# A diff-attention and convolution block on one core: seven-product pairs in the first gate/up block too, a fifth pair in the ten others, pair sums split between VectorE and GpSimd

## The chip, the cores and the metric

One core of one Trainium2 chip runs the whole block. The metric is the device time of one execution in microseconds, median of three runs. In the profile, PE is TensorE, DVE is VectorE, ACT is ScalarE, POOL is GpSimd, SP is SyncE (it issues the weight loads).

## The reference

One layer of 256 rows and 2048 columns, all in fp32. What matters for the change is the second half, the feed-forward part.

```python
h = h + jnp.einsum('bsm,md->bsd', mixed, w_out[l])        # output projection, 2048 x 2048
hn = rms_norm(h, norm2_g[l])                              # h * rstd2(row) * g2(column)
a = jnp.einsum('bsd,df->bsf', hn, w_gate[l])              # 2048 x 5632
bu = jnp.einsum('bsd,df->bsf', hn, w_up[l])               # 2048 x 5632
h = h + jnp.einsum('bsf,fd->bsd', jax.nn.silu(a) * bu, w_down[l])   # 5632 x 2048
```

Ahead of it stand a norm, an input projection to 5120 columns, differential attention with four heads, and a gated causal convolution of 31 taps over 1024 channels; `mixed` is the two side by side.

## The kernel before

**Three products for one.** TensorE multiplies in a reduced format, so each fp32 operand is split in two: `hi`, the operand cast (ScalarE, for weights), and `lo`, the rest that the cast leaves (VectorE: raw minus hi). A product is hi·hi + hi·lo + lo·hi, three matmuls. Weights therefore come in as `raw` (SP's queue), become `whi` (line 326) and `wlo` (line 335), and are multiplied. For some units the rest is made by DMA instead: ScalarE writes the negated cast's operand and GpSimd's queue adds the raw tile to it (lines 329 and 330, "by DMA" below). A load of two k-tiles (256 rows) by 512 columns is one chunk; tiles of the activations (`xhi`, `hhi`, `chi`, `ahi`) are the stationary side, weights the moving side with 512 columns.

**Gate and up in blocks of 512 columns.** The feed-forward part goes through eleven blocks j of 512 hidden columns, in groups of four, four and three; behind each group stand passes over W_down for that group (`down_pass`). A block multiplies the 256 rows by 512 columns of W_gate and the same 512 of W_up over 16 k-tiles. Except in block 0 it saves products in the manner of Strassen: two k-tiles of both weights, which are 2x2 blocks (two k-tiles by gate and up; two halves of the rows by two k-tiles), are multiplied with seven products in place of eight. Such a unit is a pair, kind "s": 21 matmuls where two plain two-k-tile units, kinds "g" and "u", have 12 each. The seven products land in eight banks of PSUM (`PRODUCTS`, `sum_bank`), into which the plain units of the block add as well; behind the last pair the banks are combined (`bank_sums`: a copy by ScalarE, line 1186, and six sums by VectorE, lines 1188 to 1193); then silu, two more sums behind the last unit (line 1209), two products (line 1214), and transposes of the result (line 898). The sevenfold operands of the activations (`fhi`, `flo`) are made once by `make_forms`.

**What a pair needs.** Its four raw tiles `wb` (two loads of 512 KB); four sums or differences of them, `wt` (lines 1049 to 1051, the third reads the second's result); two casts on ScalarE, of the three tiles used as they are (line 1052, 1536 columns) and of the four summed ones (line 1055, 2048 columns); two rests on VectorE, `wlb` (line 1058) and `wlt` (line 1059). `wb`, `wh`, `wlb` and `wlt` have two buffers each, `wt` has one.

**Block 0** is plain, because the norm's row scale `rstd2` isn't known when it starts: its 16 chunks (192 matmuls) multiply `h` times the column gains, and `rstd2` scales the sums (lines 876 and 883). Meanwhile `make_forms` spreads `rstd2` over the partitions (two transposes), scales the transposed `hn` with it, and makes the seven forms of the scaled rows.

**Order.** All units stand in one list, and `run_chunks` goes through it: ahead of unit t's matmuls it writes the casts of units up to `hi_lead` further and the rests up to `lo_lead` further (3 and 2 in the feed-forward part), loads whatever has a free buffer, and advances the side work (generators such as `bank_sums`) one step at each `resume()` that the multiplications contain. So each engine's order is the order of writing. Within a block the order of units is a string:

```python
ORDER = "sggsggsuusuu"
FIRST_ORDER = "gsggsgsuusuu"
BY_DMA = dict(g=TWOS[:2], u=TWOS[1::2])
```

Four pairs, four "g" and four "u", 180 matmuls; of the eight plain units four have their rests made by DMA, in the first block of a group only the two "u" ones.

Of the kernel before, what the change touches and what calls it, by code (L numbers as in the profile page):

```python
# [12 lines left out]
F32 = mybir.dt.float32  # L13
# [20 lines left out]
LINE = 128  # L34
EPS = 1e-6
# [29 lines left out]
RAW_BUFS = 5  # L65
# [27 lines left out]
DORDERS = {4: (ORDER, ORDER), 3: ("gguusggsuu", "gsgsgsuuu")}  # L93
# [10 lines left out]
PAIR_BUFS = 2  # L104

# [24 lines left out]
def tile_block(  # L130
# [13 lines left out]
    prestack = ExitStack()  # L144
    pre = prestack.enter_context(tc.tile_pool(name="pre", bufs=2))
    small = prestack.enter_context(tc.tile_pool(name="small", bufs=4))
# [4 lines left out]
    h = [pre.tile([P, D], F32, tag=f"h{m}", name=f"h{m}", bufs=1) for m in range(NM)]  # L151
# [255 lines left out]
    def run_chunks():  # L407
# [4 lines left out]
        loaded, split = set(), set()  # L412
# [8 lines left out]
        def split_next():  # L421
            chunks[j]["split"](chunks[j])
            split.add(j)

# [3 lines left out]
        def freed(side, t):  # L428

            which, bufs = ((raws, RAW_BUFS), (pairs, PAIR_BUFS))[side]  # L430
            if not ahead[side] or pairs[2] - 1 not in loaded:
                return None
            k = which[place[side][ahead[side][0]] - bufs]
            return k if k in split and (t >= k or not chunks[k]["by_dma"]) else None

# [7 lines left out]
        for t in range(n):  # L443
# [33 lines left out]
    def square_sum(src, accum, **kw):  # L477
        junk = pre.tile([P, N], F32, tag="junk", name="junk", bufs=1)
# [107 lines left out]
    def conv_back(b):  # L586
# [37 lines left out]
        for b in range(2):  # L624
            for t in range(NB // 2):
# [6 lines left out]
                for j in range(2):  # L632
# [3 lines left out]
                    hi = pre.tile([P, S], F32R, tag="mchi", name=f"mchi{ct}", bufs=NCT)  # L636
                    lo = pre.tile([P, S], F32R, tag="mclo", name=f"mclo{ct}", bufs=NCT)
# [135 lines left out]
    def attend_values(hd):  # L773
# [39 lines left out]
    hT = {}  # L813

    hn = []
# [9 lines left out]
    def out_done(n, ps):  # L825
        cs = slice(n * N, (n + 1) * N)
# [13 lines left out]
        for t in range(0, N // P, 2):  # L840
# [6 lines left out]
            if k % HK == 0:  # L847
                hn.append(early.tile([P, HK, S], F32, tag="wb", name="hn"))
            rows = hn[k // HK][:, k % HK : k % HK + 2, :]
            for i in range(2):  # L850
                act.activation(rows[:, i, :], pt[:, i, :], AF.Copy, scale=col("g2", k + i))
            hi, lo = lhs_two("h", k)
            act.copy(hi, rows)
            dve.tensor_tensor(lo, rows, hi.bitcast(F32), ALU.subtract)
            for i in range(2):
                hT[k + i] = (hi[:, i, :], lo[:, i, :])
# [3 lines left out]
        else:  # L860
            yield
            yield
            prestack.close()
            ffn["pool"] = ctx.enter_context(tc.tile_pool(name="ffn", bufs=1))
            start(make_forms())


    ffn = {}
    actT = {}
    sil = {}  # L870

    def silu_done(ps):
        yield
        for m in range(NM):
            sil[m] = ffn["pool"].tile([P, N], F32, tag=f"sum{m}", name="sil")
            act.activation(sil[m], ps[m], AF.Silu, scale=rstd2[m])

    def up_done(j, ps):
        fp = ffn["pool"]
        aa = []  # L880
        for m in range(NM):
            a = fp.tile([P, N], F32, tag=f"sum{2 + m}", name="a")
            dve.scalar_tensor_tensor(a, ps[m], rstd2[m], sil[m], ALU.mult, ALU.mult)
            aa.append(a)
        yield from lag(4)
        yield from transposed(j, aa)

    def transposed(j, aa):
        last = j + 1 in FIRSTS and NDS[group_of(j)[0]] < HD
        b = j - group_of(j)[1]  # L890
        for t in range(N // P // 2):
# [9 lines left out]
            if b < 2 and 2 * t < nd:  # L901
                if not b and not t:
                    raw_act[g] = ffn["pool"].tile([P, 2, nd, S], F32, tag="draw", name="raw_act")
# [30 lines left out]
    def make_down_forms(g):  # L934
# [20 lines left out]
        hs = ffn["pool"].tile([P, 2, nd, P], F32R, tag="dhs", name="dhs")  # L955
# [12 lines left out]
        ls = ffn["pool"].tile([P, 4, nd, P], F32R, tag="draw", name="dls")  # L968
# [11 lines left out]
    def make_forms():  # L980
        fp = ffn["pool"]
        rep = fp.tile([P, S], F32, tag="sum1", name="rep")
        for m in range(NM):
            act.activation(rep[:, m * P : (m + 1) * P], ident, AF.Identity, bias=rstd2[m], scale=0.0)
        yield
        ps = aux_ps.tile([P, N], F32, tag="aux", name="ps_r")
        for m in range(NM):
            pe.transpose(ps[:, m * P : (m + 1) * P], rep[:, m * P : (m + 1) * P], ident)
        yield
        rb = fp.tile([P, S], F32, tag="sum2", name="rb")  # L990
        act.copy(rb, ps[:, :S])
        yield
        for i in range(2):
            for k in range(0, HK, 4):
                t = hn[i][:, k : k + 4, :]
                dve.tensor_tensor(t, t, rb.unsqueeze(1).to_broadcast([P, 4, S]), ALU.mult)
                yield

        nr = HK - NS
        chi = fp.tile([P, 2 * nr, S], F32R, tag="chi", name="chi")  # L1000
        clo = fp.tile([P, 2 * nr, S], F32R, tag="clo", name="clo")
# [374 lines left out]
```

## Time and profile before

| What | Value |
|---|---|
| median of three runs | 1032.45 us (1032.17, 1032.45, 1032.88) |
| the profiled execution, first to last instruction | 1030.8 us (the page gives no other time for it) |
| TensorE busy | 1025.7 us, 100% |
| VectorE busy | 929.2 us, 90% |
| ScalarE busy | 643.4 us, 62% |
| GpSimd busy | 102.7 us, 10% |
| TensorE's granted clock | 1.000 over the span |
| gate/up begins, first bank copies (line 1186) | 338.3 us; 419.8 us |

The span counts from the first to the last instruction; the runs' times are longer by what lies around it, here 1.65 us for the median. The page's busy time counts an instruction from start to end, and ends of pipelined matmuls are modelled, so 100% says that TensorE always has a matmul in flight. In a view of groups or times a row reads: line, engine, operation, out<-in, shape, and in brackets the idle time ahead of it with what ended it. In the view of windows each engine has a busy time and in brackets its number of instructions, in the order PE, PEld, DVE, ACT, POOL, then the granted clock, the DMA engines' share and GB/s.

### The profile page before, as it was taken

How to read it: one execution, taken by the hardware profiler on the slowest of the kernel's cores; microseconds unless marked ns; L12 is line 12 of the kernel's file. 1: busy time of each engine (PE TensorE's matmuls, PEld its weight loads, DVE VectorE, ACT ScalarE, POOL GpSimd, SP SyncE). 2: the span in 40 equal slices, each digit the busy share in tenths (PEclk: the TensorE clock that was granted, in tenths of full speed). 3: DMA queues.
4: the chain of work that ended last, by engine and by line, in shares of the span. 5: the costliest groups of instructions: out<-in, count | busy, mean ns of one | idle time of the engine just before them, and what ended most of it. 6: DMA issues, size and time to landing. Idle time of an engine off the chain costs nothing.

```text
span 1030.8 us, 13034 instructions
## 1 busy us (share of the span) xinstructions
PE 1025.7 (100%) x4642; PEld 849.4 (82%) x4642; DVE 929.2 (90%) x1128; ACT 643.4 (62%) x786; POOL 102.7 (10%) x146
## 2 busy tenths in 40 slices
PE   9999999999999999999999999999999999999998
PEld 8888888888888888888888888888888888888887
DVE  6899999999765699999999898989999989889998
ACT  7644656665756675676666556667757556657562
POOL 0300112111000000100102101101001111010020
PEclk9999999999999999999999999999999999999999
DMA  9757555544466677997989799889798979897776
GB/s 338 254 194 258 190 184 164 158 169 166 141 215 214 197 262 222 282 265 210 254 259 272 251 257 270 258 234 262 228 269 255 285 207 283 247 267 218 226 200 174
DMA packets 116448, 238.64 MB, mean 232 GB/s; under 512 B 7840, under 2 KB 9120, under 8 KB 116384
## 3 DMA queue, kind: packets, MB, share of 16 engines
q1 hardware_dynamic: 105216, 203.58, 59.3%
q0 software_dynamic: 10880, 34.08, 17.0%
q8 instruction: 36, 0.59, 0.2%
q14 instruction: 28, 0.23, 0.1%
q10 hardware_dynamic: 288, 0.16, 0.1%
HBM read 204.24 MB, written 9.44 MB: 207 GB/s over the span
## 4 chain that ended last, share of the span: by engine, by line
PE 100%; POOL 0%; DVE 0%; issue 0%; POOLq 0%
PE acc L365 11%; PE acc L366 11%; PE acc L371 11%; PE q L1097 11%; PE q L1103 11%; PE q L1098 11%; PE q L1078 9%; PE q L1077 9%; PE q L1076 9%; PE ps_a L898 1%; PE ps_s L712 1%; PE ps_o L782 1%; PE ps_warm L164 0%; PE ps_h L846 0%; PE ps_qk L693 0%; PE ps_at L802 0%
## 5 line engine op out<-in xcount | busy, mean ns | idle before, releaser
L326 ACT CAST whi<-raw 128x1024 fp32r<-128x1024 f32 (+1 forms) x256 | 264.2, 1043 | 143.8 <-PE acc L366 86.6
L335 DVE TENSOR_TENSOR wlo<-raw,whi 128x1024 fp32r<-128x1024 f32 (+1 forms) x208 | 250.4, 1214 | 38.2 <-ACT whi L326 38.0
L1055 ACT CAST wh<-wt 128x2048 fp32r<-128x2048 f32 x61 | 116.8, 1915 | 109.9 <-DVE wt L1051 109.7
L1059 DVE TENSOR_TENSOR wlt<-wt,wh 128x2048 fp32r<-128x2048 f32 x61 | 139.8, 2291 | 19.8 <-ACT wh L1055 19.7
L1097 PE MATMUL q<-whi,chi 128*128 128x512 f32 x320 | 125.2, 391 | 0.0
L1098 PE MATMUL q<-whi,clo 128*128 128x512 f32 x320 | 124.6, 389 | 0.0
L365 PE MATMUL acc<-whi,xhi 128*128 128x512 f32 x312 | 124.1, 398 | 0.0
L366 PE MATMUL acc<-whi,xlo 128*128 128x512 f32 x312 | 122.2, 392 | 0.0
L1076 PE MATMUL q<-wh,fhi 128*128 128x512 f32 x280 | 109.8, 392 | 0.0
L1077 PE MATMUL q<-wh,flo 128*128 128x512 f32 x280 | 109.0, 389 | 0.0
L1058 DVE TENSOR_TENSOR wlb<-wb,wh 128x1536 fp32r<-128x1536 f32 x61 | 106.8, 1751 | 1.0 <-ACT wh L1052 1.0
L572 DVE SCALAR_TENSOR_TENSOR y<-upad,cw,y 128x256 f32<-128x256 f32 x240 | 101.6, 490 | 0.0
L330 POOL DMA_DIRECT2D wlo<-raw x48 | 41.5, 865 | 555.7 <-ACT wlo L329 286.3
L1052 ACT CAST wh<-wb 128x1536 fp32r<-128x1536 f32 x61 | 89.8, 1472 | 1.0 <-DMA wb<-in_w_down_dram 1.0
L1103 PE MATMUL q<-wlo,chi 128*128 128x512 f32 x320 | 85.7, 390 | 0.0
L371 PE MATMUL acc<-wlo,xhi 128*128 128x512 f32 x312 | 85.2, 394 | 0.0
L1049 DVE TENSOR_TENSOR wt<-wb 128x1024 f32<-128x1024 f32 x61 | 74.4, 1220 | 0.0
L1097 PE MATMUL q<-whi,ahi 128*128 128x512 f32 x182 | 71.0, 390 | 0.0
L1098 PE MATMUL q<-whi,alo 128*128 128x512 f32 x182 | 70.9, 389 | 0.0
L1103 PEld LDWEIGHTS q<-wlo,chi 128*128 128x128 f32 x320 | 60.0, 188 | 12.7 <-DMA wlo<-raw 0.3
L1097 PEld LDWEIGHTS q<-whi,chi 128*128 128x128 f32 x320 | 60.1, 188 | 12.3
L1098 PEld LDWEIGHTS q<-whi,clo 128*128 128x128 f32 x320 | 60.1, 188 | 12.2
(260 smaller groups left out, 1850.5 us busy)
## 6 DMA issues: line engine op xcount, KB each, us to landing
raw<-in_w_in_dram SPq DMA_DIRECT2D x78, 512.0 KB, 4.6
raw<-in_w_gate_dram SPq DMA_DIRECT2D x48, 512.0 KB, 5.0
raw<-in_w_up_dram SPq DMA_DIRECT2D x48, 512.0 KB, 5.3
wlo<-raw POOLq DMA_DIRECT2D x48, 512.0 KB, 7.1
raw<-in_w_down_dram SPq DMA_DIRECT2D x46, 512.0 KB, 6.2
wb<-in_w_down_dram SPq DMA_DIRECT2D x42, 512.0 KB, 5.9
wb<-in_w_up_dram SPq DMA_DIRECT2D x40, 512.0 KB, 4.4
wb<-in_w_gate_dram SPq DMA_DIRECT2D x40, 512.0 KB, 5.5
```

Source lines behind the costliest of these rows:

```text
L326: act.copy(c["hi"], c["raw"])
L335: dve.tensor_tensor(c["lo"], c["raw"], c["hi"].bitcast(F32), ALU.subtract)
L365: pe.matmul(ps[m], xhi[:, ms], hi[:, j, :], start=c["first"] and j == 0, stop=False)
L366: pe.matmul(ps[m], xlo[:, ms], hi[:, j, :], start=False, stop=False)
L371: pe.matmul(ps[m], xhi[:, ms], lo[:, j, :], start=False, stop=c["last"] and j == nk - 1)
L1055: act.copy(c["hi"][:, :SUMMED], c["t"])
L1059: dve.tensor_tensor(lot, c["t"], c["hi"][:, :SUMMED].bitcast(F32), ALU.subtract)
L1076: pe.matmul(ps, hi, c["hi"][:, w], start=bool(first), stop=False)
L1077: pe.matmul(ps, lo, c["hi"][:, w], start=False, stop=False)
L1097: pe.matmul(ps, xs[i][0][:, ms], hi[:, i, :], start=i == 0 and bool(c["first"].get(qs[m])), stop=False)
L1098: pe.matmul(ps, xs[i][1][:, ms], hi[:, i, :], start=False, stop=False)
L1103: pe.matmul(sum_bank(c, qs[m]), xs[i][0][:, ms], lo[:, i, :], start=False, stop=i == 1 and bool(c["last"].get(qs[m])))
```

## The change

- **Block 0** becomes a block with four pairs, by an order of its own (`ORDER0`), with the roles of the two halves of PSUM swapped. The forms are no longer scaled with `rstd2`: they are made of `h` times the gains alone, most of them during the last columns of the output projection, and every block scales behind the bank sums (silu with `scale=rstd2`, and one more scaling of its result, lines 1229 and 1230 after). `rep`, `rb` and their transposes go.
- **The ten other blocks** get a fifth pair, of k-tiles 4 and 5; the pairs are (0,8), (1,9), (2,10), (3,11) and (4,5). Three "g" and three "u" remain: 177 matmuls. The W_down passes keep their order.
- **A pair's VectorE work** is written in seven pieces, the casts of `wt` are split in two, and the second one with its rest (line 1080, in `finish_pair`) is written behind the casts of the next units.
- **GpSimd makes the three sums** of the next pair behind each `bank_sums`, where that pair's weights are loaded, its rounding isn't written yet, and the pair before is finished (`sums_aside`): 14 of 75 pairs.
- **Buffers:** four raw buffers in place of five; tiles that live on the right side of SBUF (`keep`, then `late`) take turns; the first two pairs' loads are issued five units ahead of the first unit of gate/up.

The diff, cut to its core:

```diff
-RAW_BUFS = 5
+RAW_BUFS = 4
...
-NS = 4
-REST = [k for k in range(KD) if k % HK >= NS]
+PAIRS = [(0, 8), (1, 9), (2, 10), (3, 11), (4, 5)]
+NS = len(PAIRS)
+REST = [k for k in range(KD) if not any(k in p for p in PAIRS)]
 TWOS = [tuple(REST[i : i + 2]) for i in range(0, len(REST), 2)]
-BY_DMA = dict(g=TWOS[:2], u=TWOS[1::2])
-ORDER = "sggsggsuusuu"
-FIRST_ORDER = "gsggsgsuusuu"
+BY_DMA = dict(g=TWOS[:2], u=TWOS[1:])
+ORDER = "sgsgsgsusuu"
+ORDERS = {1: "gsgsgssusuu"}
+NS0 = 4
+TWOS0 = [*PAIRS[NS0:], *TWOS]
+ORDER0 = "gugusgsgssuu"
+DOWN_ORDER = "sggsggsuusuu"
...
+PAIRS_AHEAD = 5
...
     def split_next():
         chunks[j]["split"](chunks[j])
         split.add(j)
+        if chunks[j].get("kind") == "s":
+            unfinished.append(chunks[j])
...
+            if t == first - PAIRS_AHEAD:
+                for k in pairs[:PAIR_BUFS]:
+                    load(k)
...
     def round_pair(c):
...
-        dve.tensor_tensor(t[:, 2:4], b[:, 1:3], b[:, 0:1].to_broadcast([P, 2, N]), ALU.subtract)
-        dve.tensor_tensor(t[:, 1], b[:, 1], t[:, 3], ALU.add)
-        dve.tensor_tensor(t[:, 0], t[:, 1], b[:, 3], ALU.subtract)
         act.copy(c["hi"][:, SUMMED:], b[:, 1:])
+        if "t" not in c:
+            first_sums(c, dve)
+
+    def first_sums(c, engine):
+        b = c["b"]
+        c["t"] = t = ffn["pool"].tile([P, 4, N], F32, tag="wt", name="wt")
+        engine.tensor_tensor(t[:, 2:4], b[:, 1:3], b[:, 0:1].to_broadcast([P, 2, N]), ALU.subtract)
+
+    def last_sums(c, engine):
+        b, t = c["b"], c["t"]
+        yield engine.tensor_tensor(t[:, 1], b[:, 1], t[:, 3], ALU.add)
+        yield engine.tensor_tensor(t[:, 0], t[:, 1], b[:, 3], ALU.subtract)
+
+    def sums_aside():
+        pairs = [c for c in chunks if c.get("kind") == "s"]
+        n = next((n for n, c in enumerate(pairs) if not c.get("rounded")), None)
+        if n and "b" in pairs[n] and "finished" in pairs[n - 1]:
+            c = pairs[n]
+            first_sums(c, pool)
+            c["summed"] = len(list(last_sums(c, pool)))

     def split_pair(c):
-        act.copy(c["hi"][:, :SUMMED], c["t"])
...
-        dve.tensor_tensor(lob, c["b"][:, 1:], c["hi"][:, SUMMED:].bitcast(F32), ALU.subtract)
-        dve.tensor_tensor(lot, c["t"], c["hi"][:, :SUMMED].bitcast(F32), ALU.subtract)
...
+        sums = iter(()) if c.get("summed") else last_sums(c, dve)
+        act.copy(hi[:, 2:SUMMED], t[:, 2:])
+        rest(lob[:, :1], b[:, 1:2], hi[:, SUMMED : SUMMED + 1])
+        next(sums, None)
+        rest(lob[:, 1:], b[:, 2:], hi[:, SUMMED + 1 :])
+        next(sums, None)
+        rest(lot[:, 2:], t[:, 2:], hi[:, 2:SUMMED])
...
+    def finish_pair(c):
+        hi, t = c["hi"][:, :2], c["t"][:, :2]
+        act.copy(hi, t)
+        rest(c["lot"][:, :2], t, hi)
+        c["finished"] = True
+
+    def rest(lo, raw, h):
+        dve.tensor_tensor(lo, raw, h.bitcast(F32), ALU.subtract)
...
     def bank_sums(q):
...
         dve.tensor_tensor(u3, q[Q4], u3, ALU.add)
+        sums_aside()
         return (w1, u3), (u2, w4)
     def products_done(q):
...
-        for t in g:
-            act.activation(t, t, AF.Silu)
+        for m, t in enumerate(g):
+            act.activation(t, t, AF.Silu, scale=rstd2[m])
+            act.activation(t, t, AF.Copy, scale=rstd2[m])
```

How it moves the instructions, at three places. First VectorE's order around the border of two gate/up blocks, with the bank sums of block 1 before (lines 1188 to 1193) and the pairs (lines 1049 to 1059) on both sides:

```order
L1059 TENSOR_TENSOR wlt<-wt,wh 128x2048
L1188 TENSOR_TENSOR sum_4001<-q_3731,sum_4000 128x512
L1189 TENSOR_TENSOR sum_4002<-q_3735,sum_4001 128x512
L1190 TENSOR_TENSOR sum_4003<-q_3739,sum_4002 128x512
L1191 TENSOR_TENSOR sum_4001<-q_3739,sum_4001 128x512
L1192 TENSOR_TENSOR sum_4000<-q_3706,sum_4000 128x512
L1193 TENSOR_TENSOR sum_4002<-q_3709,sum_4002 128x512
L1209 TENSOR_TENSOR sum_4001<-q_3760,sum_4001 128x512
L1209 TENSOR_TENSOR sum_4003<-q_3918,sum_4003 128x512
L1214 TENSOR_TENSOR sum_4001<-sum_4001,sum_4000 128x512
L1214 TENSOR_TENSOR sum_4003<-sum_4003,sum_4002 128x512
L1049 TENSOR_TENSOR wt<-wb 128x1024
```

and after, where block 0 is the first to have bank sums (now lines 1215 to 1220; the pair's pieces are lines 1046, 1050, 1051 and, for the rests, 1085):

```order
L1046 TENSOR_TENSOR wt<-wb 128x1024
L1215 TENSOR_TENSOR sum_3666<-q_3484,sum_3665 128x512
L1216 TENSOR_TENSOR sum_3667<-q_3488,sum_3666 128x512
L1217 TENSOR_TENSOR sum_3665<-q_3337,sum_3665 128x512
L1218 TENSOR_TENSOR sum_3668<-q_3492,sum_3667 128x512
L1219 TENSOR_TENSOR sum_3666<-q_3492,sum_3666 128x512
L1220 TENSOR_TENSOR sum_3667<-q_3340,sum_3667 128x512
L1085 TENSOR_TENSOR wlb<-wb,wh 128x512
L1050 TENSOR_TENSOR wt<-wb,wt 128x512
L1085 TENSOR_TENSOR wlb<-wb,wh 128x1024
L1051 TENSOR_TENSOR wt<-wt,wb 128x512
L1085 TENSOR_TENSOR wlt<-wt,wh 128x1024 x2
```

The six sums moved into the middle of a pair: the pair's first sum stands ahead of them, its other six pieces behind, in seven instructions of 512 and 1024 columns in place of five of up to 2048.

Second GpSimd's queue from the norm's last step into the W_down passes, before:

```order
L224 TENSOR_TENSOR rstd_138<-rsq,neghalf 128x2
L330 DMA wlo<-raw 128x1024 x15
L1242 DMA hd_85<-sum_5020 128x512
L1242 DMA hd_86<-sum_5022 128x512
L1270 DMA hd_85<-sum_5021 128x512
```

and after:

```order
L234 TENSOR_TENSOR rstd_145<-rsq,neghalf 128x2
L340 DMA wlo<-raw 128x1024 x6
L1046 TENSOR_TENSOR wt<-wb 128x1024
L1050 TENSOR_TENSOR wt<-wb,wt 128x512
L1051 TENSOR_TENSOR wt<-wt,wb 128x512
L340 DMA wlo<-raw 128x1024 x4
```

The rests by DMA (line 330, now 340) have a pair's three sums between them now, at the borders where `sums_aside` takes a pair; the lines 1242 and 1270 before add the W_down results to `h` in memory (`hd`).

Third VectorE's order where the output projection ends and gate/up begins, before:

```order
L335 TENSOR_TENSOR wlo<-raw,whi 128x1024 x7
L828 TENSOR_TENSOR h_81<-h_81,acc 128x512
L828 TENSOR_TENSOR h_82<-h_82,acc 128x512
L836 TENSOR_REDUCE ssh<-ss_0_136 128x1
L836 TENSOR_REDUCE ssh<-ss_1_137 128x1
L854 TENSOR_TENSOR hlo_3354<-hn,hhi_3353 128x512
L335 TENSOR_TENSOR wlo<-raw,whi 128x1024
L854 TENSOR_TENSOR hlo_3379<-hn,hhi_3378 128x512
```

and after:

```order
L855 TENSOR_TENSOR h_88<-h_88,acc 128x512
L855 TENSOR_TENSOR h_89<-h_89,acc 128x512
L863 TENSOR_REDUCE ssh<-ss_0_143 128x1
L863 TENSOR_REDUCE ssh<-ss_1_144 128x1
L884 SCALAR_TENSOR_TENSOR clo<-ps_h,cols,chi 128x256 x2
L1046 TENSOR_TENSOR wt<-wb 128x1024
L345 TENSOR_TENSOR wlo<-raw,whi 128x1024
L884 SCALAR_TENSOR_TENSOR clo<-ps_h,cols,chi 128x256 x2
L1085 TENSOR_TENSOR wlb<-wb,wh 128x512
L1050 TENSOR_TENSOR wt<-wb,wt 128x512
L1085 TENSOR_TENSOR wlb<-wb,wh 128x1024
L1051 TENSOR_TENSOR wt<-wt,wb 128x512
```

Behind the sums of the projection's last column (line 828, now 855) and the row sums of squares stood plain rests and the last rests of `hn`; now the first pair of block 0 stands there, with the rests of the last activation tiles (line 884) between its pieces.

More of the change, by code (lines that the diff above doesn't have):

```diff
@@ L34 @@
 LINE = 128
+EDGE = 320
 EPS = 1e-6
@@ L411, in run_chunks @@
         raws = [k for k in range(n) if chunks[k].get("kind") != "s" and not chunks[k].get("spare_raw")]
-        loaded, split = set(), set()
+        loaded, split, unfinished = set(), set(), []
+        first = min(k for k in range(n) if "kind" in chunks[k])
         def load(k):
@@ L453, in run_chunks @@
                         which.remove(i)
+                if chunks[i].get("kind") == "s":
+                    finish()
                 chunks[i]["round"](chunks[i])
@@ L825, in out_done @@
     def out_done(n, ps):
+        if not n:
+            prestack.close()
+            ffn["pool"] = fp = ctx.enter_context(tc.tile_pool(name="ffn", bufs=1))
+            ffn["rows"] = fp.tile([P, 2, NS, S], F32, tag="wh", name="hn", bufs=2)
+            for t in ("chi", "clo"):
+                ffn[t] = fp.tile([P, len(REST), S], F32R, tag=t, name=t)
         cs = slice(n * N, (n + 1) * N)
@@ L846, in out_done @@
                     pe.transpose(pt[:, i, m * P : (m + 1) * P], h[m][:, (k + i) * P : (k + i + 1) * P], ident)
[L847 to L856, printed above, removed]
+            if k not in REST:
+                for i in range(2):
+                    p, half = next((p, pair.index(k + i)) for p, pair in enumerate(PAIRS) if k + i in pair)
+                    act.activation(ffn["rows"][:, half, p, :], pt[:, i, :], AF.Copy, scale=col("g2", k + i))
+            if k in REST or k in PAIRS[NS0]:
+                a = REST.index(k) if k in REST else 0
+                hi, lo = (ffn[x][:, a : a + 2, :] for x in ("chi", "clo")) if k in REST else lhs_two("h", k)
+                for i in range(2):
+                    act.activation(hi[:, i, :], pt[:, i, :], AF.Copy, scale=col("g2", k + i))
+                for i in range(2):
+                    dve.scalar_tensor_tensor(lo[:, i, :], pt[:, i, :], col("g2", k + i), hi[:, i, :].bitcast(F32),
+                                             ALU.mult, ALU.subtract)
+                    plain[k + i] = (hi[:, i, :], lo[:, i, :])
             yield
@@ L859, in out_done @@
             h_squares(n, cs)
-        else:
+        if n == HK * P // N:
             yield
-            yield
-            prestack.close()
-            ffn["pool"] = ctx.enter_context(tc.tile_pool(name="ffn", bufs=1))
             start(make_forms())
+        if n == D // N - 1:
+            keepstack.close()
+            ffn["late"] = ctx.enter_context(tc.tile_pool(name="late", bufs=1, side="right", reuse_waits="tile"))
     ffn = {}
+    plain = {}
     actT = {}
[L870 to L886, printed above, removed]
     def transposed(j, aa):
@@ L981, in make_forms @@
         fp = ffn["pool"]
[L982 to L1001, printed above, removed]
-        for i in range(2):
-            act.copy(chi[:, i * nr : (i + 1) * nr], hn[i][:, NS:])
-        yield
@@ L1131, in multiply_two, with fast_block @@
             start(c["done"](c["sums"]))
-    def fast_block(order, pairs, twos, sources, operands, half, whole, by_dma=dict(g=(), u=())):
+    def fast_block(order, pairs, twos, sources, operands, half, whole, by_dma=dict(g=(), u=()), swap=False):
         units, sums = [], {}
@@ L1138, in fast_block @@
             what = left[kind].pop(0)
-            c = dict(kind=kind, sums=sums, done=None, first={}, last={}, rows=what["rows"], **operands)
+            c = dict(kind=kind, sums=sums, swap=swap, done=None, first={}, last={}, rows=what["rows"], **operands)
             if kind == "s":
@@ L1183, in bank_sums @@
     def bank_sums(q):
-        w1, u2, u3, w4 = (ffn["pool"].tile([P, N], F32, tag=f"sum{i}", name=f"sum{i}") for i in range(4))
+        w1, u2, u3, w4 = (ffn["late"].tile([P, N], F32, tag=f"sum{i}", name=f"sum{i}") for i in range(4))
         act.copy(w1, q[Q1])
@@ L1306, in tile_block @@
         for j in range(j0, j0 + nb):
[L1307 to L1313 removed]
+            gate_up_block(j)
         down_pass(g, j0, nb)
```

97 lines of the change are left out of this document (50 added, 47 removed).

## The prediction

> **What bounds the kernel now.** First the page: the busy table and the chain that ended last.
>
> ```profile
> span 1030.8 us, 13034 instructions
> PE 1025.7 (100%) x4642; PEld 849.4 (82%) x4642; DVE 929.2 (90%) x1128; ACT 643.4 (62%) x786; POOL 102.7 (10%) x146
> ...
> PE 100%; POOL 0%; DVE 0%; issue 0%; POOLq 0%
> ```
>
> TensorE (PE) is the bound over the whole span and waits for nobody. VectorE (DVE) is at 90% on average, so the second view is the windows from one block's bank copy to the next block's, here blocks 2, 3 and the first down pass, with the copies (line 1186) from ScalarE's timeline.
>
> ```profile
> 460.53:504.73 44.20, 44.20 (x201) 36.61 (x200) 42.09 (x44) 29.44 (x31) 3.43 (x4) 1.00 0.82 238
> 504.73:545.64 40.91, 40.91 (x186) 33.90 (x185) 39.49 (x39) 26.50 (x26) 2.62 (x3) 1.00 0.88 261
> ```
>
> ```profile
> 460.53 0.56 ACT L1186 COPY sum<-q 128x512 f32<-128x512 f32 x1
> ...
> 504.73 0.57 ACT L1186 COPY sum<-q 128x512 f32<-128x512 f32 x1
> ...
> 545.64 0.57 ACT L1186 COPY sum<-q 128x512 f32<-128x512 f32 x1
> ```
>
> Third, PE's pace from its timeline: the first matmul of two neighbouring 12-matmul chunks, and a group of four transposes.
>
> ```profile
> 332.87 0.39 PE L365 MATMUL acc<-whi,mchi 128*128 128x512 f32 x1
> ...
> 335.59 0.39 PE L365 MATMUL acc<-whi,mchi 128*128 128x512 f32 x1
> ...
> 341.03 0.67 PE L846 MATMUL ps_h<-ident,h 128*128 128x128 f32 x4
> ```
>
> A chunk takes 2.72 us, so a matmul of 512 columns 0.227; four transposes take about 0.36 (4 x 0.109 less overlap; 0.43 to the next row here). A block of today has 180 matmuls and 8 transposes, 41.5 us; yet the copies of blocks 2 and 3 lie 44.2 apart. In that stretch DVE is busy 42.1 of 44.2, its order being full with the W_down forms: DVE slipped 2.7 us behind, and PE did not stop. So some slip, at least 2.7 us, is absorbed by what is already prepared. That is the key to the change: PE gets shorter, DVE longer, in blocks where DVE is already at 95%.
>
> **DVE's own prices**, from the start of one instruction to the start of the next, since neighbours overlap by 0.08:
>
> ```profile
> 592.69 1.22 DVE L335 TENSOR_TENSOR wlo<-raw,whi 128x1024 fp32r<-128x1024 f32 x1
> 593.82 1.22 DVE L1049 TENSOR_TENSOR wt<-wb 128x1024 f32<-128x1024 f32 x1
> 595.08 0.69 DVE L1050 TENSOR_TENSOR wt<-wb,wt 128x512 f32<-128x512 f32 x1
> 595.81 0.69 DVE L1051 TENSOR_TENSOR wt<-wt,wb 128x512 f32<-128x512 f32 x1
> 596.42 1.75 DVE L1058 TENSOR_TENSOR wlb<-wb,wh 128x1536 fp32r<-128x1536 f32 x1
> 598.48 2.29 DVE L1059 TENSOR_TENSOR wlt<-wt,wh 128x2048 fp32r<-128x2048 f32 x1 [0.32 <-ACT wh L1055]
> 600.69 2.35 DVE L335 TENSOR_TENSOR wlo<-raw,whi 128x1024 fp32r<-128x1024 f32 x2
> ```
>
> A 128x1024 row costs 1.13, one of 512 0.61; an instruction that reads its forerunner's result 0.12 more (1.26, 0.73). A pair costs 6.87 (593.82 to 600.69), of it about 0.25 in two such reads and 0.32 waiting for ScalarE's cast.
>
> ```profile
> 505.76 0.69 DVE L1188 TENSOR_TENSOR sum<-q,sum 128x512 f32<-128x512 f32 x1
> 506.55 0.69 DVE L1189 TENSOR_TENSOR sum<-q,sum 128x512 f32<-128x512 f32 x1
> ...
> 509.75 1.28 DVE L1209 TENSOR_TENSOR sum<-q,sum 128x512 f32<-128x512 f32 x2
> 510.95 1.28 DVE L1214 TENSOR_TENSOR sum<-sum,sum 128x512 f32<-128x512 f32 x2
> ```
>
> The six bank sums take 4.0, the four operations behind them 2.4.
>
> **The change, part by part.**
>
> 1. *TensorE's work.* Block 0 goes from 192 to 180 matmuls, each of ten blocks from 180 to 177: 42 x 0.227 = 9.5 us less; two transposes of the old scaling row go, 0.1. Together -9.6 us, if PE never waits.
>
> 2. *A pair on DVE.* Seven instructions in place of five, interleaved (DVE's order after, in the section on the change): 4 x 1.13 + 3 x 0.61 = 6.35, no dependent neighbours; the last piece waits for the second cast (line 1080), which starts when L1051 is done and takes 1.05, about 0.07 of it uncovered: 6.4 against 6.87. Pairs back to back pay 0.12 more, since wt has one buffer. That cast stands behind the next unit's casts on ScalarE (ACT), priced here:
>
> ```profile
> L326 ACT CAST whi<-raw 128x1024 fp32r<-128x1024 f32 (+1 forms) x256 | 264.2, 1043 | 143.8 <-PE acc L366 86.6
> ```
>
> Two of them end to end, 2.1, fit beside the four DVE pieces from L1046's end to L1051 (3 x 0.61 + 1.13 = 2.96), and ScalarE is busy 62%: nothing.
>
> 3. *Sums on GpSimd*, for 14 of 75 pairs. On GpSimd's queue (the order's rows) the three sums now stand ahead of later rest DMAs (line 340). The price is not in the trace; the nearest rows are small GpSimd products beside DVE:
>
> ```profile
> 36.82 0.32 POOL L201 TENSOR_TENSOR gcsq<-rt,gb 128x64 f32<-128x64 f32 x1
> 37.10 1.30 POOL L202 TENSOR_TENSOR gcsq<-rt,gb 128x64 f32<-128x64 f32 x1
> 38.37 0.46 POOL L200 TENSOR_TENSOR gcsq<-rt,gb 128x128 f32<-128x128 f32 x1
> 38.79 0.32 POOL L201 TENSOR_TENSOR gcsq<-rt,gb 128x64 f32<-128x64 f32 x1
> ```
>
> ```profile
> 36.90 1.32 DVE L335 TENSOR_TENSOR wlo<-raw,whi 128x1024 fp32r<-128x1024 f32 x1 [1.71 <-ACT whi L326]
> 38.15 0.86 DVE L550 SCALAR_TENSOR_TENSOR u<-acc,rstd,sig 128x256 f32<-128x256 f32 x2
> ```
>
> 64 columns more cost 0.14, so 2.2 ns a column: 2.4 + 1.3 + 1.3 = 5.0 us for a pair's sums (estimate; from 2.6, DVE's own time, to 8 if each is held up once like L202). L202 took 1.30 in place of 0.32: it stood until DVE's L335, with both inputs in SBUF, was done at 38.22. L550, with an accumulator in PSUM, let L200 and L201 pass at 0.46 and 0.32. The sums start when DVE has finished the pair before, just as DVE turns to the six bank sums and the two of line 1238, which read PSUM: 5.2 us, into which 5.0 fit. So DVE saves 2.3 for such a pair (4.0 in place of 6.4) and I charge no collision outside block 3. The rest DMAs behind them on the queue belong to units two or more places later (over 7 us): nothing.
>
> The Trainium skill (SBUF — State Buffer, SBUF: two separate sides) calls the shared port "an exclusive lock, not a bandwidth split", taken by a DVE operation with two SBUF inputs; another page (Perfetto Trace Analysis, Optimizing Scalar/DVE Operations) warns that offloading between those two engines "might not help". By that rule the sum stays as it is where only PSUM readers run, and the first rival holds where they do not; both rows agree with it.
>
> 4. *Start of gate/up: block 0's first pair.* By the order's rows a whole pair now stands behind the projection's last sums (line 855, before 828) and the rests of its last four k-tiles (line 884), and PE wants it after four units. Before, seven rests were prepared ahead and nothing was due at once.
>
> ```profile
> 338.69 1.23 DVE L335 TENSOR_TENSOR wlo<-raw,whi 128x1024 fp32r<-128x1024 f32 x1 [1.49 <-ACT whi L326]
> 339.83 1.28 DVE L828 TENSOR_TENSOR h<-h,acc 128x512 f32<-128x512 f32 x2
> ...
> 341.30 0.16 DVE L836 TENSOR_REDUCE ssh<-ss 128x1 f32<-128x4 f32 x1 [0.19 <-ACT junk L479]
> ```
>
> ```profile
> 341.93 0.82 ACT L851 ACTIVATE hn<-ps_h,cols 128x256 f32<-128x256 f32 x2
> ```
>
> Gate/up begins at 338.31 (2.72 behind 335.59); call it 0. Today's first scaling (line 851) starts at +3.6 and takes 0.41 a half; with the same for the new forms' casts the two rests end at +4.9 (0.4 each, half of L550's row), then L1046 to 6.0, wlo 7.2, the second rests 8.0, the four pieces to L1051 (2.96) 10.95 and the last two 13.4. PE: four units 10.9 and the transposes 0.8, then two matmuls that need no rest, 0.45: 12.15. PE waits +1.25 (0.7 to 2). The new right-hand buffers wait for the stores of h (line 823, now 844):
>
> ```profile
> L823 POOL DMA_DIRECT2D hd<-h x8: 539/539/772, 294.2 to 341.4; - x8
> ...
> DMA to landing us min/median/max: 3.9/5.0/6.8
> ```
>
> The last is issued at 341.4 and lands in the median 5.0, at worst 6.8 later: +8.1 or +9.9, where the first rest that needs those buffers is due at +8.0. I take 0 and keep 2 for the range.
>
> 5. *Block 1*, with five pairs, three rests by DVE and no help from GpSimd. PE finishes block 0's last pair at +37.5 (6 x 2.72 + 4 x 4.77 + 0.8 + 1.25); copy 0.6, so DVE starts the sums at 38.15 and must do 4.0 (sums), 5.2 (the rest of the first pair), 2.4, three wlo 3.4, four pairs 25.6, 0.1 back to back: the last pair is ready at 78.9. PE's way there, from its last pair of block 0 to the last of block 1, is two u units, the four g and u units and four pairs ahead of it, the transposes and two matmuls that need no rest: 6 x 2.72 + 4 x 4.77 (21 x 0.227) + 0.7 + 0.45 = 36.6, so it wants the rest at 74.1. PE waits +4.8 (4 to 5.5: no buffer helps, as the sums cannot start before PE's last pair).
>
> 6. *Blocks 2 and 3, 6 and 7.* A usual block: 4 x 6.4 + 4.0 + two wlo 2.3 + 6.4 = 38.3 against PE's 177 x 0.227 + 0.7 = 40.9: hidden. Block 2 also has three W_down sums (1.8) and 0.4 back to back: 40.5, even. Block 3 carries two rests and seven W_down pieces, 9 x 0.61 more: with 0.9 for two pairs back to back and some five reads of a forerunner's result 38.3 + 5.5 + 0.9 = 44.7, and one of these reads SBUF twice in the middle of the bank sums, so it may meet GpSimd (up to 1.3). Today's rows show that 2.7 is absorbed. In group 0 the slip left by block 1 is still there, so I charge the 3.8 in excess of PE less what little is left, +3; in blocks 6 and 7, which begin with DVE ahead, +1.5. Ends: 0 (all absorbed) and 5 each. Block 10 has the smaller forms: 0. Down passes get lighter for DVE: 0.
>
> 7. *Four raw buffers, pair loads.* Pair loads are freed 9 to 11 us before need; landing
>
> ```profile
> DMA to landing us min/median/max: 3.7/5.3/11.2
> ```
>
> is 5.3 in the median, 11.2 at worst: 0, up to +2. ScalarE's two extra scalings a block: hidden.
>
> **Sum:** -9.6 + 1.25 + 4.8 + 3 + 1.5 = +1 us on the profiled span of 1030.8. The median of the runs, 1032.45, lies 1.65 above that span, so 1033.4. A change within 0.2%, 2.1 us, cannot be told from none here.
>
> **Rivals.**
>
> *GpSimd's sums block DVE* (slower). If the lock also holds readers of PSUM, or the sums start late and meet the 1024-column rests, DVE loses up to 5.0 and saves 2.3: +2.7 in each of nine gate/up blocks that get such a pair. With 38.3 to 44.7 against 40.9, about 2 us each reach PE: +18, 1050. It decides once DVE loses more than the usual block's 2.6 slack. L550's row speaks against. Half of it, two or three us in the full blocks only, gives 1038. Together 0.15.
>
> *Slip is absorbed* (faster): the prepared units cover blocks 3 and 7, as today, and block 1 loses 4: -9.6 + 1.25 + 4 = -4.3, 1028. For it: today's slip cost nothing. Against: pairs now stand at every second unit with two buffers each, so DVE cannot run far ahead. 0.27.
>
> *Pair loads come late*: at the worst landing of 11.2 in a few down-pass borders, +3 on the sum, 1036.5. DMA share is already 0.88. 0.13.
>
> *The pairs' saving holds entirely*, 1023: needs point 5 wrong. 0.05.
>
> My forecast, 1030.4 to 1036 around 1033.4: 0.40; its upper part lies beyond the 0.2%. Faster 0.31, same 0.35, slower 0.34. Range: 1025 (the absorbed case with block 0 at 0.7 and block 1 at 1.5: -9.6 + 2.2) to 1040 (the sum with both ends of 5 in point 6, +5.5, and 1 of the 2 in points 4 and 7); it leaves out the full saving and the full block of DVE.
>
> **What would show it.** Right: PE's first waits of the whole trace, on DVE's wlt (line 1085), one near 350 of about 1 us (point 4), several in block 1 adding to 5, a few in blocks 3 and 7, none in down passes; GpSimd's sums at 2.4 and 1.3 beside L1215 to L1238; DVE over 93%. Wrong: PE idle under 5 us in all; GpSimd's or DVE's rows stretched beyond these durations; waits on the pair loads.

## The result, and the profile after

The changed kernel takes 1056.9 us (median, 1055.16 to 1059.48) against 1032.43 before: 2.4% slower, ratio 1.0239 (1.0220 to 1.0257). The prediction said 1033.4 within 1025 to 1040. One execution of the run with four pairs and five raw buffers (1474.11 us, granted clock 0.655) is left out of that run's time below, and its profile is not used. The page of after:

```profile
span 1056.3 us, 13239 instructions
PE 1029.9 (97%) x4598; PEld 841.6 (80%) x4598; DVE 951.2 (90%) x1277; ACT 688.5 (65%) x876; POOL 179.2 (17%) x191
...
PE 22%; DVE 7%; DMA 4%; issue 2%; ACT 2%; POOL 0%; SPq 0%; DVEq 0%; POOLq 0%; ACTq 0%
```

The chain that ended last was TensorE throughout; now it leaves TensorE for VectorE, ScalarE and the rest DMAs. (The shares that the page gives add up to 37% of the span, so sizes are read from the waits.) What TensorE waits for, by the view of waits (in total, times, longest, in us):

```profile
PE q L1128 <- DMA wlo<-raw: 9.8, 8, 3.2
PE q L1101 <- ACT wh L1080: 5.2, 5, 3.5
PE q L1103 <- DVE wlt L1085: 2.5, 5, 0.5
...
PE acc L381 <- DVE wlo L345: 1.0, 1, 1.0
PE q L1122 <- DVE sum L1220: 1.0, 1, 1.0
PE q L1122 <- DVE sum L1217: 0.7, 1, 0.7
```

These idle times add up to some 21 us, but a stop costs more than its gap: a short one some 0.3 to 0.4 us more, and behind a long one the matmuls ran slowly. So I took the start of each unit on TensorE's timeline and subtracted 0.227 us for each matmul. The sum of what is left over in the feed-forward part is 35.6 us after and 2.1 before; with the stop of 1.0 ahead of it, that is 34.5 more, and less the 9.6 saved it gives +24.9, against the measured 25.5 of the span. By place (units that lose over 0.15 us; the rest is spread thin; predicted and measured in us):

| Place | predicted | measured |
|---|---|---|
| end of the projection, block 0 | 1.25 | 3.0 |
| block 1 | 4.8 | 3.7 |
| blocks 2 to 7 | 4.5 | 7.1 |
| blocks 8 to 10 | 0 | 1.7 |
| start of the first and second group's W_down passes | 0 | 9.3 |
| border from block 10 to the third group's passes | 0 | 2.3 |
| last pair of the kernel | 0 | 7.0 |

**The first W_down border**, from the timelines of ScalarE, GpSimd and TensorE (start, duration, engine, line):

```profile
511.60 1.06 ACT L339 ACTIVATE wlo<-raw 128x1024 fp32r<-128x1024 f32 x1 [0.16 <-PE q L1128]
```

```profile
511.40 2.73 POOL L1046 TENSOR_TENSOR wt<-wb 128x1024 f32<-128x1024 f32 x1 [1.08 <-DVE wlt L1085]
514.22 1.30 POOL L1050 TENSOR_TENSOR wt<-wb,wt 128x512 f32<-128x512 f32 x1
515.59 1.30 POOL L1051 TENSOR_TENSOR wt<-wt,wb 128x512 f32<-128x512 f32 x1
516.83 0.88 POOL L340 DMA_DIRECT2D wlo<-raw  x1
```

```profile
526.32 1.12 PE L1128 MATMUL q<-wlo,ahi 128*128 128x512 f32 x3 [2.26 <-DMA wlo<-raw]
```

The negated cast is done at 512.66, but the rest DMA stands behind the three sums on GpSimd's queue and is issued at 516.83, 4.2 us later. It lands at 526.3, and TensorE has waited 2.26. A window ahead of the stop and one behind it show the second part of its price:

```profile
515.00:522.00 7.00, 7.00 (x34) 5.80 (x34) 6.47 (x10) 6.59 (x8) 2.63 (x3) 1.00 0.99 333
...
527.20:530.20 3.00, 3.00 (x8) 2.30 (x7) 0.00 (x0) 0.00 (x0) 0.00 (x0) 0.50 0.94 303
```

Granted clock 0.50 for 3 us: 8 matmuls in place of 13. The second border repeats it, with a stop of 3.2 us, and so does the last pair of the kernel: its stop of 3.46 us ends at 1036.3, and the granted clock is 0.50 from 1035.6 to 1042.4.

**The third border**, from the timelines of VectorE and GpSimd:

```profile
971.25 4.89 DVE L985 TENSOR_TENSOR dls<-dsums,dhs 128x384 fp32r<-128x384 f32 x2
...
971.43 2.72 POOL L1046 TENSOR_TENSOR wt<-wb 128x1024 f32<-128x1024 f32 x1
...
976.06 2.31 DVE L345 TENSOR_TENSOR wlo<-raw,whi 128x1024 fp32r<-128x1024 f32 x1
```

Two operations of 384 columns, 0.55 us each when alone, took 4.89 together, and a rest of 1.22 took 2.31, while GpSimd summed: each has two inputs in SBUF. The bank sums behind them came late, and TensorE waited for them (lines 1217 and 1220).

**The last pair**, a row from the chain that ended last and one of the view of that pair's tile:

```profile
1015.93 14.54 DMA wb<-in_w_down_dram
```

```profile
DMA to landing us min/median/max: 9.2/11.9/14.5
```

The pair has two loads, issued one right behind the other. The first was issued 1.4 us behind the first adds into h in memory (`hd`, line 1271), and the second needed 14.5 us. In the kernel before the first was issued 0.3 us behind the adds, and neither took more than 9.3, by the same view of before:

```profile
DMA to landing us min/median/max: 6.9/8.1/9.3
```

### The profile page after: what moved, and what is told of

Read it like the earlier page. It is cut to its first block, busy times and chain, and to the rows that moved or that the text cites. A ratio compares the mean times of both kernels' runs of the same rounds, so it can differ in the third digit from the quotient of the medians.

```text
span 1056.3 us, 13239 instructions
## 1 busy us (share of the span) xinstructions
PE 1029.9 (97%) x4598; PEld 841.6 (80%) x4598; DVE 951.2 (90%) x1277; ACT 688.5 (65%) x876; POOL 179.2 (17%) x191
## 5 line engine op out<-in xcount | busy, mean ns | idle before, releaser
L336 ACT CAST whi<-raw 128x1024 fp32r<-128x1024 f32 (+1 forms) x228 | 237.0, 1042 | 123.6 <-PE acc L376 74.0
L345 DVE TENSOR_TENSOR wlo<-raw,whi 128x1024 fp32r<-128x1024 f32 (+1 forms) x177 | 214.3, 1219 | 37.3 <-ACT whi L336 37.1
L1085 DVE TENSOR_TENSOR wlt<-wt,wh 128x1024 fp32r<-128x1024 f32 x150 | 181.4, 1221 | 3.2 <-ACT wh L1080 3.0
L1085 DVE TENSOR_TENSOR wlb<-wb,wh 128x512 fp32r<-128x512 f32 (+1 forms) x150 | 141.6, 952 | 14.1 <-ACT wh L1039 14.0
L1101 PE MATMUL q<-wh,fhi 128*128 128x512 f32 x378 | 147.8, 391 | 1.8 <-ACT wh L1080 1.8
L1102 PE MATMUL q<-wh,flo 128*128 128x512 f32 x378 | 147.2, 389 | 0.0
L1069 ACT CAST wh<-wt 128x1024 fp32r<-128x1024 f32 x75 | 78.8, 1051 | 56.3 <-DVE wt L1046 52.4
L1080 ACT CAST wh<-wt 128x1024 fp32r<-128x1024 f32 x75 | 78.8, 1051 | 51.9 <-DVE wt L1051 48.6
L1103 PE MATMUL q<-wlt,fhi 128*128 128x512 f32 x216 | 85.1, 394 | 2.5 <-DVE wlt L1085 2.5
L1101 PEld LDWEIGHTS q<-wh,fhi 128*128 128x128 f32 x378 | 71.0, 188 | 17.5 <-ACT wh L1080 3.5
L1102 PEld LDWEIGHTS q<-wh,flo 128*128 128x128 f32 x378 | 71.0, 188 | 14.7
L1046 DVE TENSOR_TENSOR wt<-wb 128x1024 f32<-128x1024 f32 x61 | 74.4, 1220 | 8.7 <-DMA wb<-in_w_gate_dram 4.2
```

The source lines that it names most:

```text
L336: act.copy(c["hi"], c["raw"])
L345: dve.tensor_tensor(c["lo"], c["raw"], c["hi"].bitcast(F32), ALU.subtract)
L1085: dve.tensor_tensor(lo, raw, h.bitcast(F32), ALU.subtract)
L1101: pe.matmul(ps, hi, c["hi"][:, w], start=bool(first), stop=False)
L1102: pe.matmul(ps, lo, c["hi"][:, w], start=False, stop=False)
L1103: pe.matmul(ps, hi, c["lo"][w], start=False, stop=bool(last))
```

## The experiments

Three theories first: Q (GpSimd's queue and its sums), V (VectorE's load, passed on through ScalarE's casts), B (four raw buffers). The kernel before ran at 1032.5 to 1032.6 beside all of them.

### Without GpSimd's sums

```diff
-        sums_aside()
```

> The changed kernel without the sums on GpSimd (all 75 pairs' sums on VectorE). Three theories of where the 35 us went that TensorE now loses (25.5 slower plus the 9.6 saved). Theory Q (GpSimd's queue): the three sums, 5.4 us, stand ahead of the first W_down unit's rest DMA at two group borders; these two stops with the slow matmuls behind them cost 9.3 us, which go: 1048, less if VectorE has room, up to 1052 if its added 2.3 us per pair show. Theory V (VectorE's load): five pairs are too much for VectorE and through it for ScalarE's casts, so 32 us more of work on VectorE make it worse than now: above 1060. Theory B (four raw buffers): no change of the stops at the end, 1050 to 1060.

Measured 1056.83, ratio 1.0234 (1.0219 to 1.0249): no change. The time lies outside Q's range and V's and inside B's, but the trace has moved. The border stops went, as Q says, and about as much came back in waits for VectorE and ScalarE, as V says:

```profile
PE q L1101 <- ACT wh L1080: 7.6, 8, 3.7
PE q L1103 <- DVE wlt L1085: 7.4, 15, 0.5
PE q L1128 <- DMA wlo<-raw: 3.0, 3, 1.3
```

Against after, 9.8 on the rest DMAs became 3.0, 2.5 on pair rests became 7.4, and 5.2 on the casts of line 1080 became 7.6. Two effects of like size cancel, by this reading; the next runs separate them.

### Without them at the borders

```diff
-        if n and "b" in pairs[n] and "finished" in pairs[n - 1]:
+        if n and "b" in pairs[n] and "finished" in pairs[n - 1] and not (
+                pairs[n]["from"]["g"][0] is w_down and pairs[n - 1]["from"]["g"][0] is w_gate):
```

> The changed kernel, but GpSimd makes no sums where the next pair is the first of a W_down pass (the sums of these 3 pairs go to VectorE). Theory Q: the two stops at the start of a W_down pass (losses of 4.2 and 5.1 us) go and nothing else does, 1047 to 1049. Theory V: VectorE has 2.3 us more there, the stop comes back as a wait for its rests: 1053 or more. Theory B: about 1057.

Measured 1053.21, ratio 1.0191 (1.0171 to 1.0210). The edit missed two of its three places: at the first two borders the pair served is the second of the W_down pass, so only the third border's set went. With it went the wait for the bank sums there; the other two stops stayed, so this run doesn't decide between the theories. I repeated it with the condition set by the caller (its core; three sets of sums are left out):

```diff
+        if n and half == "g" and pairs[n]["from"]["g"][0] is w_down:
+            return
```

> The changed kernel, with no GpSimd sums at the three borders from gate/up to a W_down pass (11 sets of sums left of 14). The earlier try left out one of these only, the third, since at the two others the pair served is the second of the pass. Theory Q: the stops of 4.2 and 5.1 us at the first two go, and the 2.3 at the third: 1045 to 1048. Theory V: VectorE has 2.3 us more there and the stops come back in part as waits for its rests: 1049 to 1054.

Measured 1045.60, ratio 1.0130 (1.0115 to 1.0145): 11.3 us from three sets of sums, as Q has it (9.3 + 2.3). And against the run without any, the other eleven sets are worth 11.2 us. They take 24.5 us of busy time off VectorE (977.8 without any, 953.3 here), so with five pairs not quite half of that reaches TensorE, and V holds beside Q.

### The sums in the kernel before

> The kernel before with the three sums on GpSimd behind each set of bank sums, nothing else (30 sums rows, so about as many sets as in the change). Theory Q alone (the queue or the lock cost by themselves): the rest DMA at a group's border goes 3 to 4 us later, where it had 1.4 us to spare, and the sums hold up VectorE at the third border as in the change (2.3 us): 1036 to 1042. Theory V (they cost only where VectorE is late already): 1031.5 to 1033.5.

The edit moves the same three operations into a function and calls it on GpSimd behind the bank sums. Measured 1034.09, ratio 1.0015 (1.0005 to 1.0024): 1.6 us slower, below Q's range and 0.6 above V's. The rest DMAs had enough to spare, and the one stop is at the third border. VectorE's and GpSimd's timelines there:

```profile
953.48 2.72 POOL L1056 TENSOR_TENSOR wt<-wb 128x1024 f32<-128x1024 f32 x1
953.55 3.07 DVE L964 SCALAR_TENSOR_TENSOR dlo<-raw_act,dhi 128x384 fp32r<-128x384 f32 x1
```

VectorE's operation, 0.55 long, starts 0.07 behind GpSimd's and ends 0.4 behind its end (956.2): held for the whole of it. The Trainium skill (SBUF — State Buffer, SBUF: two separate sides) says that whichever starts first gets the shared port for its whole instruction; this row agrees.

### Four raw buffers in the kernel before, five in the redesign

```diff
-RAW_BUFS = 5
+RAW_BUFS = 4
```

> The kernel before with four raw buffers in place of five, nothing else. Theory B: the raw and pair loads of the last W_down pass come late, 5 us or more as in the changed kernel (6.8 lost at its last pair), 1037 to 1045. Theories Q and V: nothing but some late raw tiles that cost under 1 us, 1032 to 1033.5.

Measured 1035.36, ratio 1.0027 (1.0018 to 1.0037), 2.8 us slower: more than Q and V said, less than B, and the trace's one stop of the feed-forward part (1.0) lies at 387 us, not at the end.

### Four pairs in the redesign

```diff
-PAIRS = [(0, 8), (1, 9), (2, 10), (3, 11), (4, 5)]
+PAIRS = [(0, 8), (1, 9), (2, 10), (3, 11)]
-ORDER = "sgsgsgsusuu"
+ORDER = "sggsggsuusuu"
-ORDERS = {1: "gsgsgssusuu"}
+ORDERS = {1: "gsggsgsuusuu"}
```

(`BY_DMA` as in the kernel before.)

> The changed kernel with four pairs in every block, in the order of the kernel before (180 matmuls a block; block 0 fast as in the change; GpSimd sums, interleaved pair work and four raw buffers kept). By TensorE's work alone 2.8 us under before: 1029.6. Theory V: the stops inside gate/up (6.5 on rest DMAs, 7.9 on pair rests, most of them in blocks 0 to 3) go but for block 0's first pair: with the border stops (9.3) and the end (6.8) 1045 to 1048, without these 1031. Theory Q: 1041 to 1048, its stops at the borders stay. Theory B: the end's 6.8 stay.

Measured 1039.73, ratio 1.0070 (1.0055 to 1.0085): 17 us faster than with five, though TensorE has 6.8 us more to do. That lies below Q's range and between V's two figures. The stops inside gate/up are gone but for block 0's, and so are those at the first two borders, though the sums stand ahead of the rest DMA there too (3.4 us); it then took 5.5 to land in place of 9.5. So the wait on the queue alone doesn't make a stop: of the 11.1 us from the cast's end to TensorE's need, 3.4 and 5.5 fit, where 3.4 and 9.5 would not. Why it landed sooner here is not shown. Left are the third border (2.1) and the last pair (4.1).

> The redesign with four pairs in every block (1039.7) with five raw buffers in place of four. Theory B (raw buffers): at the end of the last W_down pass TensorE lost 4.1 us on the last pair, whose load was issued behind others; with a fifth buffer the raw loads are out earlier and the pair's load meets less traffic: 1035 to 1037. Theory L (the last pair's load is late by itself, because VectorE frees its buffer 1.1 us later than in the kernel before and the adds into h in memory are ahead of it by then): 1039 to 1040, the same 4 us lost.

Measured 1040.94, ratio 1.0084 (1.0067 to 1.0100): no gain over four raw buffers, so B falls for the end. It is 0.9 above L's range, and nothing here says why.

### The adds into h two steps later, with four pairs

```diff
-            yield from lag(HD_LAG)
+            yield from lag(HD_LAG + (2 if FGROUPS[g] == 3 else 0))
```

> The redesign with four pairs and four raw buffers; the first half's adds into h in memory in the last group's passes wait two more steps of the side work, so that the last pair's loads are issued ahead of them. Theory L: the load's second half lands 8 to 9 us behind its issue in place of 12.8, and the 4.1 us at the end shrink to under 1: 1035 to 1037. Theory B: 1039 to 1040.

Measured 1034.79, ratio 1.0022 (1.0013 to 1.0032): 4.9 us faster, and the last pairs' loads (the view of their tile) take half as long:

```profile
DMA to landing us min/median/max: 6.0/6.8/7.6
```

Theory L holds (1034.79 is just under its range): the order of the adds and the load decides.

### Both mends, with five and with four pairs

> The changed kernel (five pairs) with both mends: no GpSimd sums at the borders ahead of W_down passes (1045.6 by itself), and the last group's first adds into h two steps later. Theory L: the 4.7 us that the last pair still loses there go, 1040 to 1042; what is left above TensorE's own work (1022.9) is then VectorE's lateness in gate/up, about 15 to 17 us. Theory V's own forecast is the same number; if it comes out at 1035 or less, part of the stops in gate/up came from the end's or borders' delays, at 1045 or more the last pair is late for another reason with five pairs.

Measured 1040.76, ratio 1.0081 (1.0067 to 1.0095), as forecast.

> The redesign with four pairs and both mends. Theory K (the lock: GpSimd's sums at the third border hold VectorE's operations with two inputs in SBUF, which makes the bank sums and through them TensorE late): the 2.1 us lost at the last gate/up border go, against 1034.8 with the later adds alone: 1032 to 1033. If they stay, the bank sums are late for another reason: 1034 to 1035.

Measured 1033.13, ratio 1.0007 (0.9998 to 1.0016), 1.7 of the 2.1 us. The wait for the bank sums is gone from the trace: theory K holds.

> The redesign with four pairs and the later adds, all sums on VectorE. Theory V: with four pairs VectorE has room, so GpSimd's sums save nothing: the same as with both mends, 1032 to 1033.5. If they do save there as with five pairs (11 sets gave 11 us), it is 1036 or more.

Measured 1032.84, ratio 1.0003 (0.9994 to 1.0012): with four pairs GpSimd's sums save nothing.

### What the fifth pair costs: VectorE's load or the rest DMAs

Five pairs with both mends still lose 7.6 us against four. Two runs leave out work. The first leaves out VectorE's rests of plain units:

```diff
+        if not c["by_dma"] and c.get("kind") in ("g", "u") and c["w"] is not w_down and c["cols"][0][0]:
+            c["lo"] = c["hi"]
```

> Five pairs with both mends (1040.8); in blocks 1 to 10 the plain units whose rest VectorE makes (26 of them) multiply the cast weight twice in place of the rest: TensorE's work and all loads stay, 26 x 1.13 = 29 us of VectorE's work are left out, so the output lacks these parts. Theory V: the stops of blocks 1 to 10 (about 13 us, those on the rest DMAs among them, since ScalarE's casts for these are late when VectorE is) go but for 0 to 3 us: 1027 to 1030. Theory T: the six stops on rest DMAs (5.6 us) stay, 1033 to 1035.

Measured 1029.85, ratio 0.9974 (0.9965 to 0.9983), in V's range. The rest DMAs take as long as in the run with both mends (median 8.0 against 7.9), and still TensorE's waits for them shrink from 4.2 us

```profile
PE q L1130 <- DMA wlo<-raw: 4.2, 6, 1.1
PE q L1105 <- DVE wlt L1087: 2.5, 5, 0.5
```

to 0.5. ScalarE, whose casts come ahead of these DMAs, waits 82.3 us for VectorE's pair sums in place of 107.1:

```profile
PE q L1107 <- DVE wlt L1089: 0.9, 2, 0.5
PE q L1132 <- DMA wlo<-raw: 0.5, 1, 0.5
```

The second leaves out the rest DMAs of blocks 1 to 10, with the casts ahead of them (theory T: these DMAs cost by themselves):

> The same kernel with VectorE's rests, but the 34 units of blocks 1 to 10 whose rest is made by DMA multiply the cast weight twice instead: no negated cast on ScalarE, no rest DMA there (17 MB less traffic), and the output lacks these parts. Theory T: the stops on rest DMAs go (5.6 us) and the pair loads come earlier, 1032 to 1035. Theory V: TensorE then waits for VectorE's pair rests at nearly the same places, 1037 to 1040.

Measured 1033.95, ratio 1.0013 (1.0003 to 1.0022), in T's range: the stops on rest DMAs don't come back as waits for pair rests, which V had expected (1037 to 1040).

```profile
PE q L1107 <- DVE wlt L1089: 2.6, 5, 0.5
PE q L1105 <- ACT wh L1084: 1.5, 3, 0.8
```

So by these two runs a stop on a rest DMA comes of a late cast and of the 9 to 10 us that the DMA then needs to land: with VectorE lightened it goes though the DMAs take as long, and with the DMAs gone the waits for pair rests and their casts stay at 4.1 us in all (4.0 in the run with both mends). The second run took away the traffic, ScalarE's negated casts and the DMAs together, so how much each is worth, and whether a quicker landing alone would do, is left open.

### The pieces of a pair

In this run `round_pair` makes the three sums and `split_pair` one cast and two rests, as before.

> Five pairs with both mends, a pair's work in the form of the kernel before (three sums, one cast of the four summed tiles, two rests; 6.87 us of VectorE in place of 6.4 by the rows of the kernel before, and back to back a wait for the long cast). Theory V: 50 pairs x 0.47 = 23 us more of VectorE's time in gate/up, at the 0.36 us of the program for a us of VectorE that leaving out GpSimd's sums cost: 1047 to 1052. If the pieces don't matter, 1040 to 1042.

Measured 1055.75, ratio 1.0226 (1.0209 to 1.0243): the pieces are worth 15.0 us with five pairs, more than forecast. From pair to pair VectorE's timeline has 6.98 us with the old pieces, in block 1

```profile
399.86 1.22 DVE L1047 TENSOR_TENSOR wt<-wb 128x1024 f32<-128x1024 f32 x1
...
406.84 1.23 DVE L1047 TENSOR_TENSOR wt<-wb 128x1024 f32<-128x1024 f32 x1
```

and 6.53 with the new:

```profile
397.75 1.22 DVE L1046 TENSOR_TENSOR wt<-wb 128x1024 f32<-128x1024 f32 x1
...
404.28 1.22 DVE L1046 TENSOR_TENSOR wt<-wb 128x1024 f32<-128x1024 f32 x1
```

0.45 for each of the 75 pairs would be 34 us of VectorE at most (a few pairs have GpSimd's sums); 15 us reach the end.

### Block 0's first pair

```diff
-                   dict(g=TWOS0[2:], u=TWOS0[2:3]), swap=not j)
+                   dict(g=TWOS0[2:], u=TWOS0[1:3]), swap=not j)
```

> As the run before, and in block 0 the second u unit's rest is made by DMA too, which takes 1.13 us off VectorE ahead of block 0's first pair, where TensorE loses 1.5 to 2 us on it. Theory V for the start: 0.8 to 1.2 us less, 1031 to 1032. If the first pair is late because of the late forms and not VectorE's queue: no change.

Measured 1035.29, ratio 1.0024 (1.0014 to 1.0035): 2.2 us slower than both mends alone, against either expectation. TensorE waits for that rest DMA too (0.4) and still for the pair.

```diff
-ORDER0 = "gugusgsgssuu"
+ORDER0 = "guguusgsgssu"
```

> The redesign with four pairs, later adds and all sums on VectorE (1032.8), with block 0 in the order guguusgsgssu: its first pair one unit (2.72 us) later, one u unit in place of two behind its last pair. The stop of 1.5 us at the first pair goes; but the bank sums (4.6 us with the copy) then have 2.72 us less cover before block 1 needs the banks, which may cost up to 2 us: 1031 to 1033.5.

Measured 1034.65, ratio 1.0020 (1.0011 to 1.0029), 1.1 above the range: the stop at the pair goes and the bank sums' stops at the border to block 1 take more. No form tried that computes the whole beats the kernel before; the best, four pairs without GpSimd's sums and with the later adds, equals it.

## Why the prediction was wrong

- **TensorE's 9.6 us** (point 1): right; the 34.5 us of stops less these give the measured change of the span to within 0.6.
- **A pair at 6.4 on VectorE** (point 2): right; 6.53 back to back, 0.12 above 6.4 as said. The 5.2 us for which TensorE waits on the cast of line 1080 are places where the whole pair is late: 3.5 of them are the last pair's load.
- **GpSimd's sums** (point 3): their durations were nearly right (2.40 to 2.73, 1.29 to 1.49, 1.29 to 2.15; 5.3 a set in the mean, 5.0 forecast). "The rest DMAs behind them on the queue belong to units two or more places later (over 7 us): nothing" is **the step that failed**: at the two borders the DMA needs 9.5 and 10.3 us itself, so 11.4 us of lead (from the end of the cast at 512.66 to TensorE's need at 524.06) leave no room for 4.2 on the queue. The wait was weighed against the distance to its unit and not against that distance less the DMA's landing time. Its price is 9.3 of the 24.5 us; the run without the sums at the three borders got back 11.3 with the 2.3 of the third. The landing times stood in the trace of before, in the view of line 330:

```profile
DMA to landing us min/median/max: 5.6/7.1/10.3
```

- **The first rival** (GpSimd blocks VectorE, 1050) came nearest in size, by luck, for its mechanism is another one: PSUM readers did pass, as this bank sum beside GpSimd's sum of 2.73 us shows (0.69 before), and the lock cost 2.3 us at one place, where W_down pieces with two SBUF inputs met the sums. I had charged that to block 3 and not to the border of group 3.

```profile
513.18 0.68 DVE L1217 TENSOR_TENSOR sum<-q,sum 128x512 f32<-128x512 f32 x1
```

- **"Down passes get lighter for DVE: 0"** (point 6) and the loads of point 7: failed, 7.0 us, of which some 3 are slow matmuls behind the stop. Both looked at the pairs' usual loads; the last pair's load comes among the adds into h and the loads of h, and a slip of 1.1 us put it from 0.3 to 1.4 us behind the first of these adds. The landing of 11.2 at worst was taken from the rows of before, where the order was the other one.
- **Four raw buffers** (point 7, "0, up to +2"): 2.8 us in the kernel before; a fifth gives the redesign with four pairs nothing. Five pairs with five buffers were not tried, so what the fifth is worth there is open.
- **Starts and saturated blocks** (points 4 to 6): 10.55 predicted, 13.8 measured there; block 1's 4.8 was 3.7. But most of blocks 2 to 10 stopped on rest DMAs, not on pair rests: VectorE's lateness reaches them through ScalarE's casts. So it is in part luck that the two sums lie as near as they do.
- **A stop's price**: I counted gaps. At a rest DMA a stop costs some 0.3 to 0.4 us more (a gap of 0.49 lost 0.90, one of 0.86 lost 1.15), and the two long ones at the borders some 1.6 each for the slow matmuls.

## What to carry to other kernels

A queue that carries transfers has no slack to be read from the distance of its units alone: subtract the landing time at its slow end, then see what may stand ahead. Where two engines share a load near 95%, moving work between them can gain and lose like sums in different blocks, so remove it place by place and not as a whole. Look at the last transfers of a kernel by themselves: there a load a microsecond later than its neighbours can fall behind them all.

## What the hardware showed that I had not expected

A stop of TensorE of 2.26 us was followed by 3 us at granted clock 0.50; one of 3.0 us in the redesign with four pairs was not. The Trainium skill (TensorE: Matmul & The Clock Gate, Part 1: The HAM clock gate) puts the fall to half rate behind at least one idle window of about 3.4 us. The stop of 2.26 us is shorter, so here the measurement decides: it was enough. Why the other one was not is left open, but the traces give a hint. By windows at these borders, the clock in after is at 0.50 from 526.97 to 530.38, from 782.97 to 786.38 and from 1035.55 to 1042.38, that is for 3.41 us or twice that, and the falls lie whole multiples of 3.41 us apart. The stop of 2.26 lies within one such stretch, while a border of the stretches in the four-pair run, counted back from its clock's last change, cuts the stop of 3.0 into 1.9 and 1.0. How much of a stretch has to be idle is not shown: the second border's stop of 3.2 was cut too, into 1.2 and 2.0, and was followed by the half clock.
